# Moving operands of all projections read alternately from two places

## The chip, the cores and the metric

The kernel runs on one core of a Trainium2 chip. The metric is the device time of one execution in microseconds (us), lower is better. The core has five engines that run their own instruction streams: PE (TensorE, matmuls into PSUM, each with a weight load of its own), DVE (VectorE), ACT (ScalarE), POOL (GpSimd) and SP (SyncE, which here issues DMA transfers only).

## The reference

One encoder layer on 256 tokens of width 2048, with 16 learned meta tokens ahead of them (272 positions), all in float32:

```python
u = rms_norm(h, norm_mix[l])
proj = jnp.einsum('bld,dc->blc', u, w_in[l])
aq, ak, av, mq, mk, mv, mo, mg = jnp.split(proj, IN_SPLITS, axis=-1)
...
attn_out = diff_attention(...)
ml_out = mlstm_mixer(...)
mixed = jnp.concatenate([attn_out, ml_out.astype(attn_out.dtype)], axis=-1)
h = h + jnp.einsum('blc,cd->bld', mixed, w_out[l])
u = rms_norm(h, norm_ffn[l])
ff = jax.nn.silu(jnp.einsum('bld,df->blf', u, w_gate[l])) * jnp.einsum('bld,df->blf', u, w_up[l])
h = h + jnp.einsum('blf,fd->bld', ff, w_down[l])
...
h = rms_norm(h, norm_final)
return h[:, N_META:]
```

The head width of the differential attention is 128 (8 heads, two components of 64), that of the mLSTM 256 (4 heads, both directions). D_FF is 5632.

## The kernel before

**Arithmetic.** Every large product is made of three fp32r matmuls. An operand x is split into a high part `xh`, x rounded to fp32r, and a low part `xl`, which is x less `xh`; a product of two split operands is high by high, high by low and low by high. ACT makes the high part (a CAST), DVE or POOL the low part (a subtraction).

**Token operands.** Activations lie with their channels on the 128 partitions and tokens along the row: `uh` and `ul` hold the 16 blocks of the normalised input, 272 tokens each; `mixh[k]` and `mixl[k]` hold the mixed heads, 256 tokens; `vhl` holds high and low of the input of the feed-forward part, side by side, 256 tokens each; `ffh` and `ffl` hold its inner activations. A matmul has a stationary operand (`lhsT`, 128 columns, loaded by a weight load) and a moving one (`rhs`), whose columns stream through PE one after another; the result of moving column n goes to column n of the accumulator in PSUM.

**Projections.** `project` (L209) computes 512 output channels as four accumulators of 128 channels. It walks over the weight matrix in pieces of 256 rows by 512 columns: `load_raw` (L178) transfers a piece (512 KB) on SP's queue, `split_piece` (L195) splits it, and once two pieces are there it issues the matmuls for both. The stationary operand is a 128 by 128 block of the weights, the moving operand a block of the token operand: 272 columns for ak, av, mk and mv, 258 for mq, 256 for aq, mo and the output projection `wo`. With `both`, in gate and up (L1016 to L1042), one matmul of 512 columns multiplies the high weights with high and low tokens at once (L235), and one of 256 the low weights with the high tokens (L236); DVE adds the halves.

**First projection.** aq's first half is written out by hand (L363 to L453), with its instructions pinned: transposes of x, `x_split` (L377), which splits the transposed block out of PSUM into `uh` and `ul`, the splits of the weights, and the matmuls (`aq_matmul`, L394) follow the arrival of x. `meta_columns` (L342) does for the meta tokens what `x_split` does for x, on POOL. `gates` (L532) computes the 16 gate columns from `uh` and `ul` with a moving operand of 272 columns.

**Between the projections** run attention and the mLSTM as generators that `slot` advances. `split_mix` (L807) writes their results into `mixh` (ACT) and `mixl` (POOL). Ahead of the output projection POOL puts x together again as `uh` plus `ul` into `res` (L973). After each group of the output projection DVE adds the accumulator to `res`, ACT and DVE split the sum into `vhl` (L986, L987).

**Down.** Here the roles are turned: the stationary operand is a block of `ffh` or `ffl` (128 tokens), and the moving operand 512 columns of the split weights; `down_mm` (L1061) issues the three matmuls. In the last of the four column groups one accumulator is cut into two of 256 columns. `add_square` (L1072) adds an accumulator to `h2n`, which holds tokens on the partitions, and sums the squares for the last norm.

**Order.** Apart from pinned instructions, a scheduler with a timeline of its own places the instructions of every engine. The rows and their order are the same before and after on PE and SP; on ACT and DVE the rows and their order are the same with other shapes; on POOL two instructions become two pairs.

Of the kernel before, what the change touches and what calls it, by code (L numbers as in the profile page):

```python
# [86 lines left out]
def tile_hybrid_encoder_layer(  # L87
# [42 lines left out]
    def f(ap):  # L130
        return ap.bitcast(F32)
# [77 lines left out]
    def project(src, c0, xh, xl, n, name, kpairs=None, gain=None, hook=None, pre=(), pins=0, both=None):  # L209
        kpairs = list(range(KD // CK)) if kpairs is None else kpairs  # L210
        accs = [acc_tile(f"acc_{name}_{j}") for j in range(4)]
        pend = []
        for i, kp in enumerate(kpairs):
            if hook is not None:
                hook(i)
            elif i % 2 == 0:
                slot()
            if i < len(pre):
                wh, wl = pre[i]
            else:  # L220
                wh, wl = load_piece(src, kp * CK, c0, f"{name}_{kp}", gain, pin if i < pins else unpinned)
            pend.append((i, kp, wh, wl))
            if len(pend) < 2:
                continue
            for j in range(4):
                o = accs[j][:, :n]
                sl = slice(j * P, (j + 1) * P)
                for ii, kq, qh, ql in pend:
                    for kk in range(CK):
                        k = kq * CK + kk  # L230
                        first = ii == 0 and kk == 0
                        last = ii == len(kpairs) - 1 and kk == CK - 1
                        if both is not None:
                            pair = accs[j].rearrange("p (a n) -> p a n", a=2)
                            T.matmul(pair, lhsT=qh[:, kk, sl], rhs=both(k), start=first, stop=False)  # L235
                            T.matmul(pair[:, 1, :], lhsT=ql[:, kk, sl], rhs=xh(k), start=False, stop=last)  # L236
                            continue
                        T.matmul(o, lhsT=qh[:, kk, sl], rhs=xh(k), start=first, stop=False)  # L238
# [103 lines left out]
    def meta_columns():  # L342
        pmv = state["sc"][:, 1, :KD * NM].rearrange("p (k t) -> p k t", t=NM)
        mt = scr[:, 1024:1024 + KD * NM].rearrange("p (k t) -> p k t", t=NM)
        pin(A.copy(mt, pmv))
        G.tensor_copy(uh[:, :, :NM], mt)
        G.tensor_tensor(ul[:, :, :NM], mt, f(uh[:, :, :NM]), ALU.subtract)
        sq = scr[:, 512:512 + KD * NM].rearrange("p (k t) -> p k t", t=NM)
        G.tensor_tensor(sq, mt, mt, ALU.mult)

# [24 lines left out]
                pin(T.transpose(pm[:, m * NM:(m + 1) * NM], mn[:, m * P:(m + 1) * P], ident[:NM, :NM]))  # L375

    def x_split(d):  # L377
        pt = state[d][:, :SEQ]
        pin(A.copy(uh[:, d, NM:], pt))
        pin(V.tensor_tensor(ul[:, d, NM:], pt, f(uh[:, d, NM:]), ALU.subtract))  # L380

    def w_split(k):
        kk = k % CK
# [9 lines left out]

    def aq_matmul(j, k, term):  # L394
        wh, wl = state["wh", k // CK][:, k % CK], state["wl", k // CK][:, k % CK]
        o, sl = accs[j][:, :SEQ], slice(j * P, (j + 1) * P)
        w = wl if term == 2 else wh
        u = ul if term == 1 else uh
        pin(
            T.matmul(  # L400
                o, lhsT=w[:, sl], rhs=u[:, k, NM:],
                start=(k == 0 and term == 0), stop=(k == KD - 1 and term == 2),
            )
        )
# [127 lines left out]
    def gates():  # L532
# [4 lines left out]
        yield  # L537
        pgate = sm_tile("pgate")
        for k in range(KD):
            T.matmul(pgate[:32, :NT], lhsT=wgp[:, k, :], rhs=uh[:, k, :], start=(k == 0), stop=False)  # L540
            T.matmul(pgate[:32, :NT], lhsT=wgp[:, k, :], rhs=ul[:, k, :], start=False, stop=(k == KD - 1))
# [263 lines left out]
        return dst  # L805

    def split_mix(src, k):  # L807
        mixh[k] = kpool.tile([P, SEQ], F32R, tag="qk", bufs=32, name=f"mixh{k}")
        mixl[k] = kpool.tile([P, SEQ], F32R, tag="qk", bufs=32, name=f"mixl{k}")
# [157 lines left out]
    lp1 = left1.__enter__()  # L967
    left2 = tc.tile_pool(name="left2", bufs=1)
    lp2 = left2.__enter__()
    vhl = lp2.tile([P, KD, 2, SEQ], F32R, name="vhl")  # L970
    vh, vl = vhl[:, :, 0, :], vhl[:, :, 1, :]
    res = lp1.tile([P, KD, SEQ], F32, name="res")
    for d in range(KD):  # L973
        G.tensor_tensor(res[:, d, :], f(uh[:, d, NM:]), f(ul[:, d, NM:]), ALU.add)
    ssf = lp2.tile([P, SEQ], F32, name="ssf")
    rbf = lp2.tile([P, SEQ], F32, name="rbf")
    for g in range(4):
        accs = project(
            w_out[0], g * N_CHUNK, lambda k: mixh[k], lambda k: mixl[k], SEQ, f"wo{g}",
        )  # L980
        for j in range(4):
            d = 4 * g + j
            with tc.high_priority():
                V.tensor_tensor(res[:, d, :], accs[j][:, :SEQ], res[:, d, :], ALU.add)
            gcol = cols[:, V_GFFN + d:V_GFFN + d + 1]
            A.activation(vh[:, d, :], res[:, d, :], AF.Copy, scale=gcol)  # L986
            V.scalar_tensor_tensor(vl[:, d, :], res[:, d, :], gcol, f(vh[:, d, :]), ALU.mult, ALU.subtract)  # L987
# [27 lines left out]

    for g in range(D_FF // N_CHUNK):  # L1016
        accs = project(
            w_gate[0], g * N_CHUNK, lambda k: vh[:, k, :], None, SEQ, f"ga{g}",
            both=lambda k: vhl[:, k], hook=ffn_norm if g == 0 else None,
        )  # L1020
        sgs = []
        for j in range(4):
            s1 = fp.tile([P, SEQ], F32, tag="s1", bufs=2, name=f"s1_{g}_{j}")
            sg = fp.tile([P, SEQ], F32, tag="sg", bufs=5, name=f"sg_{g}_{j}")
            with tc.high_priority():
                add_halves(s1, accs[j])
# [4 lines left out]
        accs = project(  # L1031
            w_up[0], g * N_CHUNK, lambda k: vh[:, k, :], None, SEQ, f"up{g}",
            both=lambda k: vhl[:, k],
        )
# [25 lines left out]

    def down_mm(part, k, wh, wl, kk, pin=False):  # L1061
        acc, b, c0, n = part
        o = acc[:, :n]
        bsl = slice(b * P, (b + 1) * P)
        csl = slice(c0, c0 + n)
        mm = T.matmul(o, lhsT=ffh[:, k, bsl], rhs=wh[:, kk, csl], start=(k == 0), stop=False)  # L1066
        if pin:
            tc.keep_in_program_order(mm)
        T.matmul(o, lhsT=ffh[:, k, bsl], rhs=wl[:, kk, csl], start=False, stop=False)  # L1069
        T.matmul(o, lhsT=ffl[:, k, bsl], rhs=wh[:, kk, csl], start=False, stop=(k == KF - 1))  # L1070

    def add_square(part, n0, col):  # L1072
        acc, b, c0, n = part
        ysl = slice(n0 + c0, n0 + c0 + n)
        V.tensor_tensor(h2n[:, b, ysl], acc[:, :n], h2n[:, b, ysl], ALU.add)
# [96 lines left out]
```

## Time and profile before

| | |
|---|---|
| Time, median of 3 runs | 1198.35 us (1198.05 to 1199.13) |
| Time of the profiled execution | 1198.92 us |
| Its span | 1197.1 us |
| PE, weight loads | 7629 records each |
| DVE, ACT, POOL | 1153, 1179, 313 instructions |
| DMA | 212.85 MB, mean 178 GB/s |
| Granted clock of the core, mean | 0.998 |

The profiled execution was recorded by the hardware profiler; the median is of runs without it. Its page gives busy times of each engine, the chain of work that ended last, and groups of instructions by line, operation and tile. "Busy" for PE covers the whole time from the start of a matmul to its modelled end, and successive matmuls overlap, so PE at 99% doesn't say at what pace it works. A group row holds line, engine and operation, output and inputs, active rows and columns, shape, count, then busy time, the mean time of one in ns and the idle time of the engine ahead of it. Some matmul records can be missing from a trace.

The stages by their first and last matmul on the timeline: input projections with attention and mLSTM up to 356 us, output projection to 448 us, gate and up to 939 us, down to 1189 us, and the end of the last norm with the output.

### The profile page before, as it was taken

The page shows a single profiled execution, that of the slowest core. Times are in us where ns is not written, and L with a number is a line of the kernel's source. Part 1 is how long each engine was busy: PE and PEld are TensorE (multiplying, and loading weights), DVE is VectorE, ACT ScalarE, POOL GpSimd, SP SyncE. Part 2 cuts the span into 40 slices and gives each one's busy share as a digit, 9 for nine tenths or more (in the row PEclk, how much of TensorE's full clock was granted, in tenths as well). Part 3 has the DMA queues.
Part 4 walks back from the last instruction along what each step waited for, and adds up shares of the span by engine and source line. Part 5 has one row for each costly group of instructions (what it writes and reads, how often), then busy time and mean ns, then how long its engine had stood idle before and what let it go on. Part 6 is the DMA issues. An engine that isn't in the chain of part 4 may idle for free.

```text
span 1197.1 us, 19833 instructions
## 1 busy us (share of the span) xinstructions
PE 1184.0 (99%) x7629; PEld 1073.5 (90%) x7629; DVE 731.3 (61%) x1153; ACT 649.5 (54%) x1179; POOL 241.6 (20%) x313
## 2 busy tenths in 40 slices
PE   9999999999999999999999999999999999999997
PEld 8999999999999998888888888888888888888896
DVE  6887877887766566555655655665554544444444
ACT  6568768678965344554554454454554534343433
POOL 7220130010227633122122122122132100000000
PEclk9999999999999999999999999999999999999999
DMA  8555455454445655565665665655655755555563
GB/s 270 164 156 160 138 153 150 141 145 139 140 142 178 196 189 178 183 203 177 193 195 177 200 187 177 210 178 176 211 179 174 251 189 186 186 186 185 182 187 103
DMA packets 112255, 212.85 MB, mean 178 GB/s; under 512 B 8906, under 2 KB 9744, under 8 KB 112016
## 3 DMA queue, kind: packets, MB, share of 16 engines
q1 hardware_dynamic: 111664, 210.48, 57.0%
q8 instruction: 60, 0.98, 0.3%
q10 hardware_dynamic: 176, 1.06, 0.3%
q14 instruction: 35, 0.29, 0.1%
q0 software_dynamic: 320, 0.04, 0.0%
HBM read 209.45 MB, written 2.10 MB: 177 GB/s over the span
## 4 chain that ended last, share of the span: by engine, by line
PE 93%; DVE 3%; DMA 1%; ACT 1%; issue 1%; SPq 0%; POOL 0%; ACTq 0%; DVEq 0%; POOLq 0%
PE acc_up L235 14%; PE acc_ga L235 14%; PE acc_ga L236 7%; PE acc_up L236 7%; PE acc_dn L1066 7%; PE acc_dn L1070 7%; PE acc_dn L1069 7%; PE acc_wo L239 3%; PE acc_wo L240 3%; PE acc_wo L238 3%; PE acc_mv L238 1%; PE acc_mv L240 1%; PE acc_mv L239 1%; PE acc_mo L240 1%; PE acc_mo L238 1%; PE acc_mo L239 1%
## 5 line engine op out<-in xcount | busy, mean ns | idle before, releaser
L235 PE MATMUL acc_ga<-vhl,wh_ga 128*128 128x512 f32 x704 | 240.8, 394 | 0.0
L235 PE MATMUL acc_up<-vhl,wh_up 128*128 128x512 f32 x704 | 240.5, 394 | 0.0
L200 DVE TENSOR_TENSOR wl_dn<-raw_dn,wh_dn 128x1024 fp32r<-128x1024 f32 x88 | 108.2, 1230 | 133.3 <-ACT wh_dn L199 133.3
L236 PE MATMUL acc_ga<-vhl,wl_ga 128*128 128x256 f32 x704 | 187.0, 280 | 0.0
L236 PE MATMUL acc_up<-vhl,wl_up 128*128 128x256 f32 x704 | 186.5, 280 | 0.0
L200 DVE TENSOR_TENSOR wl_up<-raw_up,wh_up 128x1024 fp32r<-128x1024 f32 x88 | 115.0, 1337 | 91.0 <-ACT wh_up L199 91.0
L199 ACT CAST wh_dn<-raw_dn 128x1024 fp32r<-128x1024 f32 x88 | 92.2, 1049 | 142.7 <-PE acc_dn L1070 130.9
L200 DVE TENSOR_TENSOR wl_ga<-raw_ga,wh_ga 128x1024 fp32r<-128x1024 f32 x88 | 106.1, 1236 | 79.4 <-ACT wh_ga L199 79.4
L235 PEld LDWEIGHTS acc_ga<-vhl,wh_ga 128*128 128x128 f32 x704 | 129.9, 188 | 26.2
L235 PEld LDWEIGHTS acc_up<-vhl,wh_up 128*128 128x128 f32 x704 | 129.9, 188 | 26.2
L1070 PE MATMUL acc_dn<-wh_dn,ffl 128*128 128x512 f32 (+1 forms) x396 | 146.8, 371 | 0.0
L1066 PE MATMUL acc_dn<-wh_dn,ffh 128*128 128x512 f32 (+1 forms) x396 | 146.7, 371 | 0.0
L1069 PE MATMUL acc_dn<-wl_dn,ffh 128*128 128x512 f32 (+1 forms) x396 | 146.4, 370 | 0.0
L236 PEld LDWEIGHTS acc_up<-vhl,wl_up 128*128 128x128 f32 x704 | 132.2, 189 | 3.8
L236 PEld LDWEIGHTS acc_ga<-vhl,wl_ga 128*128 128x128 f32 x704 | 132.2, 189 | 3.6
L199 ACT CAST wh_ga<-raw_ga 128x1024 fp32r<-128x1024 f32 x88 | 89.1, 1049 | 81.4 <-PE acc_ga L235 41.8
L199 ACT CAST wh_up<-raw_up 128x1024 fp32r<-128x1024 f32 x88 | 89.0, 1048 | 68.9 <-PE acc_ga L235 36.8
L1070 PEld LDWEIGHTS acc_dn<-wh_dn,ffl 128*128 128x128 f32 x396 | 74.5, 188 | 13.7
L1069 PEld LDWEIGHTS acc_dn<-wl_dn,ffh 128*128 128x128 f32 x396 | 74.5, 188 | 13.7
L1066 PEld LDWEIGHTS acc_dn<-wh_dn,ffh 128*128 128x128 f32 x396 | 74.5, 188 | 13.4
L239 PE MATMUL acc_wo<-mixl,wh_wo 128*128 128x256 f32 x256 | 72.2, 282 | 0.0
L240 PE MATMUL acc_wo<-mixh,wl_wo 128*128 128x256 f32 x256 | 71.9, 281 | 0.0
(365 smaller groups left out, 2607.0 us busy)
## 6 DMA issues: line engine op xcount, KB each, us to landing
raw_ga<-in_w_gate_dram SPq DMA_DIRECT2D x88, 512.0 KB, 4.4
raw_up<-in_w_up_dram SPq DMA_DIRECT2D x88, 512.0 KB, 4.5
raw_dn<-in_w_down_dram SPq DMA_DIRECT2D x88, 512.0 KB, 4.2
raw_wo<-in_w_out_dram SPq DMA_DIRECT2D x32, 512.0 KB, 4.0
raw_ak<-in_w_in_dram SPq DMA_DIRECT2D x16, 512.0 KB, 4.2
raw_av<-in_w_in_dram SPq DMA_DIRECT2D x16, 512.0 KB, 4.0
raw_mv<-in_w_in_dram SPq DMA_DIRECT2D x16, 512.0 KB, 3.9
raw_mo<-in_w_in_dram SPq DMA_DIRECT2D x16, 512.0 KB, 4.0
```

The source lines that it names most:

```text
L199: pin(A.copy(wh, raw))
L200: pin(V.tensor_tensor(wl, raw, f(wh), ALU.subtract))
L235: T.matmul(pair, lhsT=qh[:, kk, sl], rhs=both(k), start=first, stop=False)
L236: T.matmul(pair[:, 1, :], lhsT=ql[:, kk, sl], rhs=xh(k), start=False, stop=last)
L238: T.matmul(o, lhsT=qh[:, kk, sl], rhs=xh(k), start=first, stop=False)
L239: T.matmul(o, lhsT=qh[:, kk, sl], rhs=xl(k), start=False, stop=False)
L240: T.matmul(o, lhsT=ql[:, kk, sl], rhs=xh(k), start=False, stop=last)
L1066: mm = T.matmul(o, lhsT=ffh[:, k, bsl], rhs=wh[:, kk, csl], start=(k == 0), stop=False)
L1069: T.matmul(o, lhsT=ffh[:, k, bsl], rhs=wl[:, kk, csl], start=False, stop=False)
L1070: T.matmul(o, lhsT=ffl[:, k, bsl], rhs=wh[:, kk, csl], start=False, stop=(k == KF - 1))
```

## The change

Each token operand is stored as two halves in each of its blocks: even tokens in the first half, odd tokens in the second. `uh` and `ul` get the shape (128, 16, 2, 136), `mixh[k]` and `mixl[k]` (128, 2, 128), `vhl` (128, 16, 2, 2, 128). The matmuls read the halves by turns (`woven`): first token 0 from the first half, then token 1 from the second, then token 2 from the first, 512 or 544 bytes apart. So the accumulators hold the tokens in the old order, and what follows them is as before; only their view is given as pairs. The instructions that write the operands read their source with a step of two words (`apart`) and write the two halves; POOL's two instructions for the meta tokens become two for each half. The sum for `res` reads the halves and writes with a step of two.

In down the storage of the weights stays. A matmul's 512 (or 256) moving columns are read by turns from the left and the right half of the column group (`woven(halves(...))`), 1,024 (or 512) bytes apart, and the accumulator holds the columns in that order; `add_square` reads it with a step of two words and adds it to the two halves of the row of `h2n`.

Stationary operands, the number of matmuls and their columns, transfers and pools stay. The core of the diff:

```diff
-    uh = lowp.tile([P, KD, NT], F32R, name="uh")
-    ul = lowp.tile([P, KD, NT], F32R, name="ul")
+    HT, HM, HS = NT // 2, NM // 2, SEQ // 2
+    uh = lowp.tile([P, KD, 2, HT], F32R, name="uh")
+    ul = lowp.tile([P, KD, 2, HT], F32R, name="ul")
+
+    def woven(ap):
+        return ap.rearrange("p r n -> p n r")
+
+    def pairs(ap):
+        return ap.rearrange("p (n r) -> p n r", r=2)
+
+    def apart(ap):
+        return ap.rearrange("p (n r) -> p r n", r=2)
+
+    def halves(ap):
+        return ap.rearrange("p (r n) -> p r n", r=2)
...
@@ project
-                o = accs[j][:, :n]
+                o = pairs(accs[j][:, :n])
...
-                            pair = accs[j].rearrange("p (a n) -> p a n", a=2)
+                            pair = accs[j].rearrange("p (a n r) -> p a n r", a=2, r=2)
                             T.matmul(pair, lhsT=qh[:, kk, sl], rhs=both(k), start=first, stop=False)
-                            T.matmul(pair[:, 1, :], lhsT=ql[:, kk, sl], rhs=xh(k), start=False, stop=last)
+                            T.matmul(pair[:, 1], lhsT=ql[:, kk, sl], rhs=xh(k), start=False, stop=last)
...
@@ in_proj
-            w_in[0], c0, lambda k: uh[:, k, t0:], lambda k: ul[:, k, t0:], NT - t0, name, gain=gm, **kw
+            w_in[0], c0, lambda k: woven(uh[:, k, :, t0 // 2:]), lambda k: woven(ul[:, k, :, t0 // 2:]),
+            NT - t0, name, gain=gm, **kw
...
@@ meta_columns
-        G.tensor_copy(uh[:, :, :NM], mt)
-        G.tensor_tensor(ul[:, :, :NM], mt, f(uh[:, :, :NM]), ALU.subtract)
+        for r in range(2):
+            G.tensor_copy(uh[:, :, r, :HM], mt[:, :, r::2])
+            G.tensor_tensor(ul[:, :, r, :HM], mt[:, :, r::2], f(uh[:, :, r, :HM]), ALU.subtract)
...
@@ x_split
-        pt = state[d][:, :SEQ]
-        pin(A.copy(uh[:, d, NM:], pt))
-        pin(V.tensor_tensor(ul[:, d, NM:], pt, f(uh[:, d, NM:]), ALU.subtract))
+        pt = apart(state[d][:, :SEQ])
+        pin(A.copy(uh[:, d, :, HM:], pt))
+        pin(V.tensor_tensor(ul[:, d, :, HM:], pt, f(uh[:, d, :, HM:]), ALU.subtract))
...
@@ split_mix
-        A.copy(mixh[k], src)
-        G.tensor_tensor(mixl[k], src, f(mixh[k]), ALU.subtract)
+        A.copy(mixh[k], apart(src))
+        G.tensor_tensor(mixl[k], apart(src), f(mixh[k]), ALU.subtract)
...
-        G.tensor_tensor(res[:, d, :], f(uh[:, d, NM:]), f(ul[:, d, NM:]), ALU.add)
+        G.tensor_tensor(apart(res[:, d, :]), f(uh[:, d, :, HM:]), f(ul[:, d, :, HM:]), ALU.add)
...
-            A.activation(vh[:, d, :], res[:, d, :], AF.Copy, scale=gcol)
-            V.scalar_tensor_tensor(vl[:, d, :], res[:, d, :], gcol, f(vh[:, d, :]), ALU.mult, ALU.subtract)
+            rd = apart(res[:, d, :])
+            A.activation(vh[:, d], rd, AF.Copy, scale=gcol)
+            V.scalar_tensor_tensor(vl[:, d], rd, gcol, f(vh[:, d]), ALU.mult, ALU.subtract)
...
-            w_gate[0], g * N_CHUNK, lambda k: vh[:, k, :], None, SEQ, f"ga{g}",
-            both=lambda k: vhl[:, k], hook=ffn_norm if g == 0 else None,
+            w_gate[0], g * N_CHUNK, lambda k: woven(vh[:, k]), None, SEQ, f"ga{g}",
+            both=lambda k: vhl[:, k].rearrange("p a r n -> p a n r"), hook=ffn_norm if g == 0 else None,
...
@@ down_mm
-        o = acc[:, :n]
+        o = pairs(acc[:, :n])
         bsl = slice(b * P, (b + 1) * P)
-        csl = slice(c0, c0 + n)
-        mm = T.matmul(o, lhsT=ffh[:, k, bsl], rhs=wh[:, kk, csl], start=(k == 0), stop=False)
+        ph, pl = (woven(halves(w[:, kk, c0:c0 + n])) for w in (wh, wl))
+        mm = T.matmul(o, lhsT=ffh[:, k, bsl], rhs=ph, start=(k == 0), stop=False)
...
@@ add_square
-        V.tensor_tensor(h2n[:, b, ysl], acc[:, :n], h2n[:, b, ysl], ALU.add)
+        y = halves(h2n[:, b, ysl])
+        V.tensor_tensor(y, apart(acc[:, :n]), y, ALU.add)
```

The up projection, the output projection, `aq_matmul` and the gate matmuls are changed in the same way as those shown.

More of the change, by code (lines that the diff above doesn't have):

```diff
@@ L395, in aq_matmul @@
         wh, wl = state["wh", k // CK][:, k % CK], state["wl", k // CK][:, k % CK]
-        o, sl = accs[j][:, :SEQ], slice(j * P, (j + 1) * P)
+        o, sl = pairs(accs[j][:, :SEQ]), slice(j * P, (j + 1) * P)
         w = wl if term == 2 else wh
@@ L400, in aq_matmul @@
             T.matmul(
-                o, lhsT=w[:, sl], rhs=u[:, k, NM:],
+                o, lhsT=w[:, sl], rhs=woven(u[:, k, :, HM:]),
                 start=(k == 0 and term == 0), stop=(k == KD - 1 and term == 2),
@@ L539, in gates @@
         for k in range(KD):
-            T.matmul(pgate[:32, :NT], lhsT=wgp[:, k, :], rhs=uh[:, k, :], start=(k == 0), stop=False)
-            T.matmul(pgate[:32, :NT], lhsT=wgp[:, k, :], rhs=ul[:, k, :], start=False, stop=(k == KD - 1))
+            o = pairs(pgate[:32, :NT])
+            T.matmul(o, lhsT=wgp[:, k, :], rhs=woven(uh[:, k]), start=(k == 0), stop=False)
+            T.matmul(o, lhsT=wgp[:, k, :], rhs=woven(ul[:, k]), start=False, stop=(k == KD - 1))
         gsb = kpool.tile([32, NT + 2], F32, tag="t1", bufs=5, name="gsb")
@@ L807, in split_mix @@
     def split_mix(src, k):
-        mixh[k] = kpool.tile([P, SEQ], F32R, tag="qk", bufs=32, name=f"mixh{k}")
-        mixl[k] = kpool.tile([P, SEQ], F32R, tag="qk", bufs=32, name=f"mixl{k}")
-        A.copy(mixh[k], src)
-        G.tensor_tensor(mixl[k], src, f(mixh[k]), ALU.subtract)
+        mixh[k] = kpool.tile([P, 2, HS], F32R, tag="qk", bufs=32, name=f"mixh{k}")
+        mixl[k] = kpool.tile([P, 2, HS], F32R, tag="qk", bufs=32, name=f"mixl{k}")
+        A.copy(mixh[k], apart(src))
+        G.tensor_tensor(mixl[k], apart(src), f(mixh[k]), ALU.subtract)
     def attention(h0, nh):
@@ L969, in tile_hybrid_encoder_layer @@
     lp2 = left2.__enter__()
-    vhl = lp2.tile([P, KD, 2, SEQ], F32R, name="vhl")
-    vh, vl = vhl[:, :, 0, :], vhl[:, :, 1, :]
+    vhl = lp2.tile([P, KD, 2, 2, HS], F32R, name="vhl")
+    vh, vl = vhl[:, :, 0], vhl[:, :, 1]
     res = lp1.tile([P, KD, SEQ], F32, name="res")
     for d in range(KD):
-        G.tensor_tensor(res[:, d, :], f(uh[:, d, NM:]), f(ul[:, d, NM:]), ALU.add)
+        G.tensor_tensor(apart(res[:, d, :]), f(uh[:, d, :, HM:]), f(ul[:, d, :, HM:]), ALU.add)
     ssf = lp2.tile([P, SEQ], F32, name="ssf")
@@ L978, in tile_hybrid_encoder_layer @@
         accs = project(
-            w_out[0], g * N_CHUNK, lambda k: mixh[k], lambda k: mixl[k], SEQ, f"wo{g}",
+            w_out[0], g * N_CHUNK, lambda k: woven(mixh[k]), lambda k: woven(mixl[k]), SEQ, f"wo{g}",
         )
@@ L1031, in tile_hybrid_encoder_layer @@
         accs = project(
-            w_up[0], g * N_CHUNK, lambda k: vh[:, k, :], None, SEQ, f"up{g}",
-            both=lambda k: vhl[:, k],
+            w_up[0], g * N_CHUNK, lambda k: woven(vh[:, k]), None, SEQ, f"up{g}",
+            both=lambda k: vhl[:, k].rearrange("p a r n -> p a n r"),
         )
@@ L1062, in down_mm @@
         acc, b, c0, n = part
-        o = acc[:, :n]
+        o = pairs(acc[:, :n])
         bsl = slice(b * P, (b + 1) * P)
-        csl = slice(c0, c0 + n)
-        mm = T.matmul(o, lhsT=ffh[:, k, bsl], rhs=wh[:, kk, csl], start=(k == 0), stop=False)
+        ph, pl = (woven(halves(w[:, kk, c0:c0 + n])) for w in (wh, wl))
+        mm = T.matmul(o, lhsT=ffh[:, k, bsl], rhs=ph, start=(k == 0), stop=False)
         if pin:
             tc.keep_in_program_order(mm)
-        T.matmul(o, lhsT=ffh[:, k, bsl], rhs=wl[:, kk, csl], start=False, stop=False)
-        T.matmul(o, lhsT=ffl[:, k, bsl], rhs=wh[:, kk, csl], start=False, stop=(k == KF - 1))
+        T.matmul(o, lhsT=ffh[:, k, bsl], rhs=pl, start=False, stop=False)
+        T.matmul(o, lhsT=ffl[:, k, bsl], rhs=ph, start=False, stop=(k == KF - 1))
     def add_square(part, n0, col):
```

## The prediction

> **What bounds the kernel now.** I read the page's busy shares first, then the chain of work that ended last.
>
> ```profile
> PE 1184.0 (99%) x7629; PEld 1073.5 (90%) x7629; DVE 731.3 (61%) x1153; ACT 649.5 (54%) x1179; POOL 241.6 (20%) x313
> ...
> PE 93%; DVE 3%; DMA 1%; ACT 1%; issue 1%; SPq 0%; POOL 0%; ACTq 0%; DVEq 0%; POOLq 0%
> ```
>
> PE (TensorE) is busy for 99% of the span, and 93% of the chain is PE. The profiled execution took 1198.92 us, 0.6 us over the median of the runs (1198.35); the sum below is made against 1198.92. Next, the stretches of the program: input projections with attention and the mLSTM, output projection, gate and up, down. Each row holds the length, then busy time and count (x) of PE, of its weight loads, of DVE, ACT and POOL, then the granted clock, the DMA share and GB/s.
>
> ```profile
> 37.30:356.30 319.00, 317.20 (x2556) 310.73 (x2555) 250.40 (x591) 234.80 (x578) 54.49 (x81) 1.00 0.52 149
> 356.30:447.90 91.60, 91.60 (x778) 91.60 (x777) 58.86 (x70) 43.12 (x60) 51.44 (x51) 1.00 0.57 182
> 447.90:938.80 490.90, 490.90 (x2824) 430.96 (x2823) 280.02 (x320) 240.29 (x353) 102.04 (x135) 1.00 0.60 189
> 938.80:1188.60 249.80, 249.80 (x1218) 207.62 (x1216) 114.35 (x111) 103.10 (x126) 9.75 (x9) 1.00 0.57 180
> ```
>
> PE has no gap in the three later projections, and 1.8 us of gaps in the first (319.00 less 317.20). The clock is 1.00 in all four. Next come the two longest waits of PE.
>
> ```profile
> PE pw L292 <- POOL ones L139: 1.4, 1, 1.4
> PE acc_av L238 <- DVE ak L802: 0.8, 1, 0.8
> ```
>
> None is over 1.4 us. So the time is a number of matmuls times the distance from one start to the next, and only that distance is worth looking at. The timeline of gate, start in us first:
>
> ```profile
> 600.91 0.39 PE L235 MATMUL acc_ga<-vhl,wh_ga 128*128 128x512 f32 x1
> 601.14 0.28 PE L236 MATMUL acc_ga<-vhl,wl_ga 128*128 128x256 f32 x1
> 601.26 0.39 PE L235 MATMUL acc_ga<-vhl,wh_ga 128*128 128x512 f32 x1
> 601.49 0.28 PE L236 MATMUL acc_ga<-vhl,wl_ga 128*128 128x256 f32 x1
> ```
>
> A matmul of 512 columns starts 0.23 us before its successor (600.91 to 601.14, 601.26 to 601.49), one of 256 columns 0.12 (601.14 to 601.26). What do columns cost? The groups by shape give finer numbers; the mean time of one is the last number before the second bar.
>
> ```profile
> L235 PE MATMUL acc_ga<-vhl,wh_ga 128*128 128x512 f32 x704 | 240.8, 394 | 0.0
> L236 PE MATMUL acc_ga<-vhl,wl_ga 128*128 128x256 f32 x704 | 187.0, 280 | 0.0
> ...
> L706 PE MATMUL pst<-mqT,mkT 128*128 128x256 f32 x16 | 4.1, 379 | 0.0
> ...
> L1113 PE MATMUL ph<-ident,res 128*128 128x128 f32 x32 | 5.3, 271 | 0.0
> ```
>
> The recorded duration is the distance plus a constant: 394 less 230 is 164. Taking 164 off all rows, L236 has 116 ns for 256 columns. Then 230 less 116 is 114 ns for the other 256 columns, 0.445 ns a column. L706 and L1113 aren't fp32r but plain fp32, where one instruction leaves several records: 379 less 164 is 215 ns for 256 columns, 271 less 164 is 107 for 128, 0.84 ns a column without any remainder. Half of that is 0.42. So **an fp32r column costs 0.45 ns where the fp32 rows, at half the pace, make 0.42 likely: about 7% of every projection is a stall that grows with the columns**, and is missing where the moving operand is read half as fast. That is the only loss left in PE that I can see.
>
> The Trainium skill, TensorE: Matmul & The Clock Gate, section "Wait — 56ns, not 53.3ns?", states a start-to-start distance of N divided by 2.4 GHz plus about 2.5 ns, 216 ns for 512 columns; the trace disagrees for fp32r (230) and agrees in the fp32 row (215 for 256 columns, a distance that it would give to 512). By it the sum below would be the same within 2 us.
>
> **The change, part by part.** The instructions of every engine stay in their order, and no wait or DMA is added. What changes is where operands lie and in what order they are read.
>
> *1. Matmuls (all of the projections, and the 32 for the gates).* The operand that streams through PE is no longer read from consecutive words. Column 0 comes from one block, column 1 from another 512 to 1,024 bytes away, column 2 from the first again. Counts, stationary operand, PSUM order and number of columns stay. The trace has no matmul that reads this way, so the cost of a column is bounded from both sides by the nearest rows. Below: 0.42 ns (the stall is gone). Above: 0.84 ns (each column costs what it costs in L706, the slowest streaming row). I take the lower end and set out why under the rivals. Distances now, from windows that hold one kind of work:
>
> ```profile
> 360.00:440.00 80.00, 80.00 (x680) 80.00 (x679) 50.71 (x53) 37.67 (x52) 49.02 (x47) 1.00 0.58 184
> 500.00:900.00 400.00, 400.00 (x2301) 351.19 (x2300) 225.61 (x252) 196.20 (x288) 80.87 (x108) 1.00 0.60 189
> 945.00:1125.00 180.00, 180.00 (x785) 145.38 (x784) 81.76 (x70) 72.07 (x82) 5.39 (x4) 1.00 0.60 191
> ```
>
> Gate and up: 400.00 us for 2301 matmuls, 173.8 ns each, 347.7 for a pair of 512 and 256. Output projection: 80.00 by 680 is 117.6 ns. Down: 180.00 us less 20 transposes of 0.107 is 177.9, by 765 is 232.5 ns. The input projections I take from the groups, less 164:
>
> ```profile
> L238 PE MATMUL acc_mv<-uh,wh_mv 128*128 128x272 f32 x128 | 37.5, 294 | 0.0
> ...
> L238 PE MATMUL acc_mo<-uh,wh_mo 128*128 128x256 f32 x128 | 36.2, 283 | 0.0
> ...
> L876 PE MATMUL po<-val,aT 128*128 128x128 f32 x32 | 6.2, 275 | 0.0
> ```
>
> That is 130 ns for 272 columns, stretched where other matmuls come between (by L236, 0.445 ns for each of 16 more columns make 123; I use 127, the middle), and 119 for 256. The matmuls of 258 columns are counted with these, those of 256 in down's tail with the output projection. What stands in the way of 0.42 a column in short matmuls is the weight load that each has: L876, 128 columns with a new stationary operand every time, has 275 less 164, 111 ns, though its columns need 107. I take 111 as the floor of a 256-column matmul, 117 for 272 and 215 for 512. The sum:
> - gate and up: 1408 pairs by (347.7 less 326) 21.7 ns, 30.6 us
> - down, 512 columns: 924 by 17.5 ns, 16.2 us
> - output projection and down's tail: 768 and 264 by 6.6 ns, 6.8 us
> - input projections of 272 columns (ak, av, mk, mv): 1344 by 10 ns, 13.4 us
> - of 256 or 258 (mo, mq, the second half of aq): 768 by 8 ns, 6.1 us; the first half of aq runs while data arrive, and is left out
>
> Together 73.1 us. With 107.5 in place of 111 as the floor (and 114 for 272) each of the 4552 matmuls below 512 columns gives 3.5 ns more: 89.
>
> *2. What covers it.* A faster PE waits for weights. In the first long stretch DVE is busy 250.40 of 319 us; with 24 us less that is 85%, and ACT (234.80) 80%. Between its bursts PE will sometimes wait there; the gaps of today are 1.8 us, and I put 4 more at it. Gate and up leave DVE at 61% of 460 us, down at 50%, and the DMA share rises from 0.60 to 0.64: nothing there becomes the bound. Left, rounded: **70 us**.
>
> *3. Operands written apart.* The splits that write the operands read every second word:
>
> ```profile
> L974 POOL TENSOR_TENSOR res<-uh,ul 128x256 f32<-128x256 f32 x16 | 18.9, 1219 | 0.1
> ...
> L987 DVE SCALAR_TENSOR_TENSOR vhl<-res,cols,vhl 128x256 fp32r<-128x256 f32 x16 | 12.3, 766 | 0.6 <-ACT vhl L986 0.6
> L380 DVE TENSOR_TENSOR ul<-ptx,uh 128x256 fp32r<-128x256 f32 x16 | 6.8, 423 | 3.7 <-ACT uh L379 3.2
> L1075 DVE TENSOR_TENSOR h2n<-acc_dn,h2n 128x512 f32<-128x512 f32 x7 | 4.5, 684 | 3.3 <-PE acc_dn L1070 3.3
> ...
> L986 ACT ACTIVATE vhl<-res,cols 128x256 fp32r<-128x256 f32 x16 | 7.8, 503 | 8.6 <-DVE res L984 8.6
> L379 ACT CAST uh<-ptx 128x256 fp32r<-128x256 f32 x16 | 5.9, 366 | 3.5 <-PE ptx L371 3.5
> ```
>
> Times if each were to take twice as long (the far end; the near end is nothing): L379 and L380 12.7 us in the first 37 us on two engines that are two thirds busy, of which perhaps 3 reach PE; L986 and L987 20.1 us beside the output projection, where DVE has 33 us free of 91.6; L974 18.9 on POOL, needed only at the end of each output group. L1075 is on the path once, at the end, with 0.4 us. I take 0 and keep 4 us for the range. On POOL two instructions become four:
>
> ```profile
> L347 POOL TENSOR_TENSOR ul<-scr,uh 128x256 fp32r<-128x256 f32 x1 | 0.7, 738 | 0.1
> L346 POOL CAST uh<-scr 128x256 fp32r<-128x256 f32 x1 | 0.4, 387 | 0.0
> ```
>
> Half as long each plus a start, so at most 1.1 us more, inside the stretch that waits for x; nothing.
>
> **Rivals.**
>
> *A, forecast: the stall goes.* For it: the loss is proportional to columns (114 against 116 ns for each 256), independent of which tensor is read (gate reads vhl, which nobody writes; down reads weights that ACT and DVE write beside it; 230 against 232.5), and absent at half the reading pace. So it is a limit of reading one place after another, and two places by turns is what could relieve it. 1198.9 less 70 is **1129**. Own range 1110 (floor 107.5) to 1165 (half of the gain).
>
> *B, slower: the second place costs a fetch of its own.* Consecutive words share what is fetched; read by turns, each column might need a fetch. Place: every projection matmul. Price with the far end, 0.84 a column: gate and up 1408 pairs by (645 less 347.7) 419 us; down 924 by 197.5, 182; output projection and down's tail 1032 by 97.4, 101; the input projections 1344 by 101.5 and 960 by 96, 229. Together 931 us: **2130**; if half of the columns pay, 1664. It decides as soon as a column costs over 0.453 ns (347.7 by 768). Against it: PE reads two far places already, the moving operand and the next weights, and the matmuls of 256 columns, which load the same weights in half the time, lose no more per column than those of 512. For it: no row shows a scattered read at full pace. The Trainium skill, SBUF — State Buffer, section "Specifications (TRN2)", speaks for it: lines of 16 bytes need at least two hits for full bandwidth, and each crossing to a new line pays. No row here shows such a crossing by turns; contiguous fp32r crosses every fourth column.
>
> *C, no difference.* The 7% is not in reading the moving operand but, say, in writing PSUM or in an fp32r step of the array. Then only part 3 is left: 1199, up to 1203. For it: the trace cannot tell those from reading, since L706 differs in kind of arithmetic as well as in pace.
>
> *D, a mild loss.* C, and the strided splits cost what part 3 bounds, or PE's short matmuls lose a few ns at the start: 2430 thousand columns are read, and a hundredth more of them is 11 us: 1210.
>
> **How the numbers follow.** A 0.64, with everything down to a small gain; C 0.15; B 0.16; D 0.05. Within 0.2% (2.4 us, about what a measurement of this kernel can tell from no change): 0.15; faster 0.64; slower 0.21. The range reaches from A's lower end, 1110, over C to 1205; it leaves out B, most of D and a little of A, under 2 in 10.
>
> **What would show it.** A: gate's 512 columns near 379 ns recorded in place of 394, its 256 columns near 275, the row of 500 to 900 us with some 2450 matmuls, PE still without gaps after the input projections. B: the same rows near 594 and 379, DVE and ACT half idle. C: rows unchanged to 2 ns. Part 2 is wrong if PE waits for wh and wl by more than 10 us in sum; part 3 if L379, L380 or L987 grow by over a third and a wait for them is among PE's longest. The prediction fails altogether if the stall is the array's own.

## The result and the profile after

The changed kernel takes 1133.8 us (median of 4 runs, 1133.51 to 1134.18) against 1198.46 us for the kernel before, a ratio of 0.946 with a 95% interval of 0.9444 to 0.9477. The profiled execution has a span of 1132.3 us, 64.8 us less than before.

The page's busy times and the chain by engine, of the kernel after:

```profile
PE 1114.3 (98%) x7629; PEld 1043.5 (92%) x7629; DVE 730.0 (64%) x1153; ACT 649.6 (57%) x1179; POOL 244.5 (22%) x315
...
PE 91%; DVE 5%; DMA 2%; issue 1%; ACT 1%; SPq 0%; POOL 0%; ACTq 0%; DVEq 0%; POOLq 0%
```

PE still fills the span. It runs the same 7629 matmul records in less time, so the distance from one start to the next has shrunk on the mean. Where the time went shows in the same stretches as before, cut at the first matmul of each stage (length, then busy time and count of PE, weight loads, DVE, ACT, POOL, then clock, DMA share, GB/s):

```profile
37.60:343.00 305.40, 299.36 (x2556) 292.95 (x2556) 250.00 (x591) 233.19 (x578) 56.19 (x81) 1.00 0.53 156
343.00:429.60 86.60, 86.60 (x778) 86.60 (x777) 59.61 (x70) 44.20 (x60) 53.67 (x51) 1.00 0.60 192
429.60:891.60 462.00, 462.00 (x2824) 424.82 (x2824) 277.13 (x319) 240.52 (x351) 101.47 (x136) 1.00 0.63 201
891.60:1123.70 232.10, 232.10 (x1218) 206.81 (x1216) 115.18 (x112) 103.45 (x128) 9.71 (x10) 1.00 0.60 194
```

Output projection 91.60 to 86.60, gate and up 490.90 to 462.00, down 249.80 to 232.10: 5.0, 28.9 and 17.7 us less, with PE free of gaps in all three as before. The input projections fall from 319.00 to 305.40, while PE's busy time in them falls from 317.20 to 299.36: 17.8 us of work are gone and the gaps grow from 1.8 to 6.0 us. The groups by shape carry the distances (mean time of one in ns ahead of the second bar):

```profile
L248 PE MATMUL acc_ga<-vhl,wh_ga 128*128 128x512 f32 x704 | 227.4, 382 | 0.0
...
L249 PE MATMUL acc_ga<-vhl,wl_ga 128*128 128x256 f32 x704 | 182.1, 273 | 0.0
...
L1083 PE MATMUL acc_dn<-wh_dn,ffh 128*128 128x512 f32 x308 | 117.2, 381 | 0.0
...
L251 PE MATMUL acc_wo<-mixh,wh_wo 128*128 128x256 f32 x256 | 70.3, 275 | 0.0
...
L251 PE MATMUL acc_mv<-uh,wh_mv 128*128 128x272 f32 x128 | 36.2, 284 | 0.0
...
L251 PE MATMUL acc_av<-uh,wh_av 128*128 128x272 f32 x128 | 35.9, 282 | 2.1 <-DVE ak L818 2.0
...
L251 PE MATMUL acc_mo<-uh,wh_mo 128*128 128x256 f32 x128 | 35.4, 277 | 0.0
```

Less 164, as in the prediction, these are 218 ns for 512 columns in gate (230 before), 109 for 256; 217 for 512 columns in down; 111 and 113 for 256 in the output projection and mo; 118 to 120 for 272 in ak, av and mv, where interruptions stretch the mean. An uninterrupted pair of gate and up comes to 327 ns:

```profile
500.00:850.00 350.00, 350.00 (x2140) 321.82 (x2139) 208.00 (x235) 183.48 (x268) 72.96 (x99) 1.00 0.64 202
```

350.00 us by half of 2140. The longest waits of PE, after:

```profile
PE pat L877 <- DVE e L870: 3.0, 2, 1.8
PE acc_av L251 <- DVE ak L818: 2.0, 1, 2.0
PE pw L306 <- POOL ones L139: 1.4, 1, 1.4
PE ptx L386 <- DMA xn<-in_x_dram: 0.9, 1, 0.9
PE acc_aq L415 <- DVE ul L395: 0.5, 1, 0.5
PE acc_av L253 <- DVE wl_av L206: 0.4, 1, 0.4
```

The same wait of the transposes before, at 0.5 us:

```profile
PE pat L861 <- DVE e L854: 0.5, 1, 0.5
```

The new gaps are this wait of the transposes of attention for its softmax weights (`e`), 2.5 us longer, and the one of av's first matmul for the rope of ak, 1.2 us longer; waits for split weights (`wl`) stay below half a microsecond. The groups of the splits that now read with a step of two words:

```profile
L1003 ACT ACTIVATE vhl<-res,cols 128x256 fp32r<-128x256 f32 x16 | 9.2, 595 | 8.7 <-DVE res L1000 8.6
L1004 DVE SCALAR_TENSOR_TENSOR vhl<-res,cols,vhl 128x256 fp32r<-128x256 f32 x16 | 13.1, 820 | 1.0 <-ACT vhl L1003 1.0
L990 POOL TENSOR_TENSOR res<-uh,ul 128x256 f32<-128x256 f32 x16 | 19.6, 1268 | 0.1
L395 DVE TENSOR_TENSOR ul<-ptx,uh 128x256 fp32r<-128x256 f32 x16 | 6.8, 422 | 3.2 <-ACT uh L394 2.4
```

L1003 was 503 ns, L1004 766, L990 1219, L395 423. None is near twice its time.

### The profile page after: what moved, and what is told of

Read it like the earlier page. It is cut to its first block, busy times and chain, and to the rows that moved or that the text cites. A ratio compares the mean times of both kernels' runs of the same rounds, so it can differ in the third digit from the quotient of the medians.

```text
span 1132.3 us, 19840 instructions
## 1 busy us (share of the span) xinstructions
PE 1114.3 (98%) x7629; PEld 1043.5 (92%) x7629; DVE 730.0 (64%) x1153; ACT 649.6 (57%) x1179; POOL 244.5 (22%) x315
## 4 chain that ended last, share of the span: by engine, by line
PE 91%; DVE 5%; DMA 2%; issue 1%; ACT 1%; SPq 0%; POOL 0%; ACTq 0%; DVEq 0%; POOLq 0%
PE acc_up L248 14%; PE acc_ga L248 14%; PE acc_ga L249 7%; PE acc_up L249 7%; PE acc_dn L1086 7%; PE acc_dn L1083 7%; PE acc_dn L1087 7%; PE acc_wo L251 3%; PE acc_wo L252 3%; PE acc_wo L253 3%; PE acc_mv L251 1%; PE acc_mv L252 1%; PE acc_mv L253 1%; PE acc_mo L253 1%; PE acc_mo L251 1%; PE acc_mo L252 1%
## 5 line engine op out<-in xcount | busy, mean ns | idle before, releaser
L248 PE MATMUL acc_ga<-vhl,wh_ga 128*128 128x512 f32 x704 | 227.4, 382 | 0.0
L248 PE MATMUL acc_up<-vhl,wh_up 128*128 128x512 f32 x704 | 227.0, 382 | 0.0
L249 PE MATMUL acc_ga<-vhl,wl_ga 128*128 128x256 f32 x704 | 182.1, 273 | 0.0
L249 PE MATMUL acc_up<-vhl,wl_up 128*128 128x256 f32 x704 | 181.6, 273 | 0.0
L1083 PE MATMUL acc_dn<-wh_dn,ffh 128*128 128x512 f32 (+1 forms) x396 | 141.2, 357 | 0.0
L1087 PE MATMUL acc_dn<-wh_dn,ffl 128*128 128x512 f32 (+1 forms) x396 | 141.2, 357 | 0.0
L1086 PE MATMUL acc_dn<-wl_dn,ffh 128*128 128x512 f32 (+1 forms) x396 | 140.9, 356 | 0.0
L212 ACT CAST wh_up<-raw_up 128x1024 fp32r<-128x1024 f32 x88 | 88.8, 1047 | 57.0 <-PE acc_ga L248 30.6
L1057 POOL TENSOR_TENSOR sg<-up,sg 128x256 f32<-128x256 f32 x44 | 33.4, 759 | 174.1 <-DVE up L1031 174.0
```

Source lines behind the costliest of these rows:

```text
L212: pin(A.copy(wh, raw))
L249: T.matmul(pair[:, 1], lhsT=ql[:, kk, sl], rhs=xh(k), start=False, stop=last)
L1083: mm = T.matmul(o, lhsT=ffh[:, k, bsl], rhs=ph, start=(k == 0), stop=False)
L1086: T.matmul(o, lhsT=ffh[:, k, bsl], rhs=pl, start=False, stop=False)
L1087: T.matmul(o, lhsT=ffl[:, k, bsl], rhs=ph, start=False, stop=(k == KF - 1))
```

## The experiments

The stages show that reading by turns is faster. They don't show why, and three explanations fit them: that successive columns come from places that lie apart (theory "place" below), that the operand is described in several dimensions ("form"), or that each new line of memory costs something and two lines can stay open ("line"). In down the order of the moving columns can be chosen freely in each of four column groups, since the storage of the weights stays and the addition of the accumulator undoes the order. So each kernel of the first kind below has three orders in the first three groups (of 264 matmuls of 512 columns each) and leaves the rest of the kernel after as it is. PE does the same arithmetic and writes PSUM in the same order in all of them. Each of these five kernels was run once; the groups of one run are compared with each other and with the distances above. What is compared is the mean distance between starts: the length of a window inside the group, by three times the count of one of the three lines, good to one per cent. (The recorded duration of the slow orders is longer than the distance by more than 164, so it isn't used.)

**Plain, in pairs, 8 bytes apart.** Written out for the third group (the kernel takes the order of each group from a table):

```diff
@@ down_mm
-        ph, pl = (woven(halves(w[:, kk, c0:c0 + n])) for w in (wh, wl))
+        ph, pl = (w[:, kk, c0:c0 + n].rearrange("p (n r j) -> p n j r", r=2, j=2) for w in (wh, wl))
@@ add_square
-        V.tensor_tensor(y, apart(acc[:, :n]), y, ALU.add)
+        V.tensor_tensor(y, acc[:, :n].rearrange("p (n j r) -> p n r j", r=2, j=2), y, ALU.add)
```

where `y` has the form "p n r j" too. The others differ in r and j only.

> The kernel after, with another reading order in the first three column groups of down (the fourth stays as after): group 0 reads its 512 moving columns plainly, as before; group 1 reads the same consecutive words, but described in pairs (steps 2 and 1); group 2 reads words 0, 2, 1, 3 of every four, so the two places lie 8 bytes apart. Theory 'place' (the stall comes from consecutive columns lying in the same small unit of memory): group 0 at 232 ns a matmul, group 1 the same 232, group 2 still near 232 as long as the unit is 16 bytes or more. Theory 'form' (an operand described in several dimensions escapes the stall): 232, 216, 216. Whole kernel: place 1133.8 plus 3 times 4.4 is 1147, form 1138.

The three rows of this kernel, one for each group, from windows of 60 us (892 to 952), 57 us (957 to 1014) and 57 us (1019 to 1076):

```profile
L1130 PE MATMUL acc_dn<-wh_dn,ffh 128*128 128x512 f32 x86 | 33.9, 396 | 0.0
L1130 PE MATMUL acc_dn<-wh_dn,ffh 128*128 128x512 f32 x81 | 32.1, 396 | 0.0
L1130 PE MATMUL acc_dn<-wh_dn,ffh 128*128 128x512 f32 x82 | 32.5, 396 | 0.0
```

60 us by 258 is 233 ns, 57 by 243 is 235, 57 by 246 is 232; the kernel took 1147.3 us. With the first three groups back at the old distance the kernel is 13.5 us slower than after. The second group tells nothing new: pairs that follow one another were merged, and its operand is the same plain row of 512 words. The third is a real operand of three dimensions, whose columns also come from two places by turns, and it is as slow as plain reading. "Form" falls, and with it the idea that any two places read by turns would do: 8 bytes are too near. "Place" had expected this.

**16, 32 and 64 bytes apart** (j = 4, 8, 16 in the diff above).

> As the run with 8 bytes, with the two places 16, 32 and 64 bytes apart in groups 0, 1 and 2 of down. Theory 'place': 216 ns a matmul from the distance on that is larger than the unit; if the unit is a line of 16 bytes (the Trainium skill, SBUF — State Buffer, names such lines) all three groups are at 216, if it is larger the first one or two stay at 232. Theory 'line' (each new line costs, two places only escape because their lines stay open): 216 in all three. Theory 'form': 216 in all three. Whole kernel 1134 to 1143.

The first two groups, from windows of 56 us each (892 to 948, 950 to 1006); the row of the third (1008 to 1064) reads like the second's:

```profile
L1130 PE MATMUL acc_dn<-wh_dn,ffh 128*128 128x512 f32 x86 | 32.5, 380 | 0.0
L1130 PE MATMUL acc_dn<-wh_dn,ffh 128*128 128x512 f32 x87 | 33.1, 380 | 0.0
```

56 us by 258 is 217 ns, by 261 it is 215, and the kernel took 1133.8 us, as after. From 16 bytes on it makes no difference how far apart the places lie. For "place" this would make the unit 16 bytes; "line" had expected 216 ns here too.

**128 bytes apart; a step of 8; a step of 16 bytes.** The second group reads all even words and then all odd ones, the third every fourth word in four passes (again written out):

```diff
@@ down_mm
+        # r = 256, j = 2 (second group); r = 128, j = 4 (third group)
+        ph, pl = (w[:, kk, c0:c0 + n].rearrange("p (r j) -> p j r", r=r) for w in (wh, wl))
```

> Group 0 of down: two places 128 bytes apart. Group 1: words read with a step of two (8 bytes), first all even, then all odd. Group 2: words read with a step of four (16 bytes), four passes, so every column lies in a new 16-byte line and none is read twice in a row. Theory 'place': 216 in group 0; in groups 1 and 2 consecutive columns leave the unit sooner than plain reading does, so 216 to 232 in group 1 and 216 in group 2. Theory 'line': 216 in group 0, 232 or more in group 1, and about 430 in group 2 (the kernel then takes 57 us longer, 1191). Theory 'form': 216 in all.

Windows of 55 us (892 to 947), 117 us (950 to 1067) and 119 us (1071 to 1190):

```profile
L1130 PE MATMUL acc_dn<-wh_dn,ffh 128*128 128x512 f32 x84 | 31.8, 380 | 0.0
L1130 PE MATMUL acc_dn<-wh_dn,ffh 128*128 128x512 f32 x86 | 55.7, 648 | 0.0
L1130 PE MATMUL acc_dn<-wh_dn,ffh 128*128 128x512 f32 x86 | 57.0, 663 | 0.0
```

55 us by 252 is 218 ns; 117 by 258 is 453; 119 by 258 is 461. The kernel took 1261.1 us. Theory "place" expected 216 to 232 ns for the step of 8 and 216 for the step of 16, and is wrong by a factor of two. "Line" had 232 or more and about 430, and 1191 us for the kernel: it foresaw that the step of 16 would be slow, not that the step of 8 would be as slow. A step of two words halves the pace, although it touches each line of 16 bytes twice in a row, just as plain reading touches it four times.

**Four places; runs of two words; a step of 32 bytes** (r = 4, j = 128; two places 1,024 bytes apart, two words at a time; r = 64, j = 8 in groups of 512).

> Group 0 of down: four places by turns, 512 bytes apart. Group 1: two places 1,024 bytes apart... read in runs of two words (256 bytes of words each side in turn of 8 bytes). Group 2: a step of eight words (32 bytes). Theory 'place': 216 in group 0 and 216 in group 2; in group 1 every second column still follows its neighbour, so half of the stall, about 224. Theory 'line': 430 in group 2, 216 or more in group 0 if only two lines stay open. Theory 'form': 216 in all.

Windows of 72 us (892 to 964), 84 us (967 to 1051) and 111 us (1055 to 1166):

```profile
L1130 PE MATMUL acc_dn<-wh_dn,ffh 128*128 128x512 f32 x86 | 38.2, 446 | 0.0
L1130 PE MATMUL acc_dn<-wh_dn,ffh 128*128 128x512 f32 x86 | 43.1, 502 | 0.0
L1130 PE MATMUL acc_dn<-wh_dn,ffh 128*128 128x512 f32 x86 | 53.4, 621 | 0.0
```

279, 326 and 430 ns; the kernel took 1236.7 us. "Place" had 216, about 224 and 216, and misses all three; "line" had the 430. The runs of two words are the telling row: only two places are open, and still it is 50% slower than after (326 against 217).

These four kernels suggested a new theory, which the next one was made to test: even and odd columns are fetched by a reader each. With two readers most orders sort themselves by one number, how many words of a line of 16 bytes one reader takes in a row. Plain reading gives words 0 and 2 of a line to one reader, 1 and 3 to the other: two. The order 0, 2, 1, 3 gives 0 and 1 to one, 2 and 3 to the other: two again. By turns from places 16 bytes apart or more: four. A step of 8 bytes: words 0, 4, 8 to one reader, one of each line. Two orders don't fit: with four places, and with runs of two words, a reader takes one word and comes to the same line again later, and they took 279 and 326 ns, far less than the 453 of the step of 8. In this theory the unit has to be 16 bytes: with units of 8, plain reading and the step of 8 would be alike (one word each), with units of 32, plain reading and places 16 bytes apart (four words each).

**Runs of four words; by turns with a step of 8; by turns with a step of 16 bytes.** Shortened:

```diff
@@ down_mm
+        # first group: "r n w" read as "n r w", r = 2, w = 4
+        # second and third group: "r n m" read as "m n r", r = 2, m = 2 or 4
+        held, read, sizes = ...  # of the group
+        ph, pl = (w[:, kk, c0:c0 + n].rearrange(f"p ({held}) -> p {read}", **sizes) for w in (wh, wl))
```

> Two theories are left after the first four kernels. 'Lanes': even columns and odd columns are fetched apart, each by a reader of its own that holds one line of 16 bytes; a column is free of stall where its reader takes all four words of a line in a row, costs about 0.45 ns with two words in a row, and about 0.87 with one. 'Two places': what counts is that each column lies far from the one before it and that no more than two places are visited by turns. The kernel after, with three other orders in down. Group 0: two places 1,024 bytes apart, read in runs of four words; each reader takes two words of a line in a row. Lanes: 232 ns a matmul, as in plain reading. Two places: more than 216 and like the runs of two words (327) or between. Group 1: two places by turns, each read with a step of two words (8 bytes); each reader takes two words of a line in a row. Lanes: 232. Two places: 216. Group 2: two places by turns, each read with a step of four words (16 bytes); each reader takes one word of a line. Lanes: about 450. Two places: 216. Whole kernel: lanes 1134 plus 4.2, 4.2 and 62, that is 1204; two places 1134 to 1163.

Windows of 64 us (893 to 957), 59 us (960 to 1019) and 116 us (1023 to 1139):

```profile
L1087 PE MATMUL acc_dn<-wh_dn,ffh 128*128 128x512 f32 x86 | 35.6, 416 | 0.0
L1087 PE MATMUL acc_dn<-wh_dn,ffh 128*128 128x512 f32 x84 | 33.3, 396 | 0.0
L1087 PE MATMUL acc_dn<-wh_dn,ffh 128*128 128x512 f32 x86 | 55.7, 647 | 0.0
```

64 us by 258 is 248 ns, 59 by 252 is 234, 116 by 258 is 450; the kernel took 1210.7 us. The second and third group read from two places by turns, 1,024 bytes apart, exactly as after does, only with larger steps within each place. Theory "two places" had 216 for both; they came out at 234 and 450, as "lanes" had it. The first group is 7% slower than the 232 that "lanes" expected, and the kernel 7 us slower than its 1204.

All orders together, with the words of a line that one reader takes in a row:

| order of the 512 columns | words in a row per reader | ns |
|---|---|---|
| two places by turns, 16 to 128 or 1,024 bytes apart | 4 | 215 to 218 |
| plain; 0, 2, 1, 3 | 2 | 232 to 235 |
| two places by turns, step of 8 bytes in each | 2 | 234 |
| runs of four words from two places by turns | 2, next line far away | 248 |
| four places by turns | 1, returns to the line | 279 |
| runs of two words from two places by turns | 1, returns to the line | 326 |
| step of 32 bytes | 1 | 430 |
| two places by turns, step of 16 bytes in each | 1 | 450 |
| step of 8 bytes, of 16 bytes | 1 | 453, 461 |

One reader with one open line is excluded: reading by turns would be its worst case. One reader with two open lines is excluded by the runs of two words. The three rows between 240 and 330 ns, in which a reader leaves a line and goes to a distant one, are explained by neither theory in size (by the prices of "lanes" they would be at 232 and twice at about 450), and what they cost was not settled. So it is shown that the order of reading sets the distance; that two readers with a line each are behind it is inferred from the times, with these three rows open, and no record shows the readers.

**Down alone.** The kernel before, with `woven(halves(...))` in `down_mm` and the matching addition in `add_square`, all else as before.

```diff
@@ down_mm of the kernel before
-        csl = slice(c0, c0 + n)
+        ph, pl = (woven(halves(w[:, kk, c0:c0 + n])) for w in (wh, wl))
```

> The kernel before, with only the moving operands of down read by turns; token operands and the other projections as before. The gain of each stage stands by itself: the down stage falls from 249.8 us to 232.1 as in the whole change, nothing else moves, 1198.5 less 17.7 is 1180.8 us, ratio 0.985. Rival: part of down's gain hangs on the earlier stages (its first weights arrive sooner, or the DMA has less to catch up), then the stage is longer than 233 us and the kernel over 1182.

1181.2 us (1180.79 to 1181.68), ratio 0.9856 with an interval of 0.9839 to 0.9872. The stage in one row:

```profile
939.00:1171.10 232.10, 232.10 (x1218) 206.74 (x1216) 114.32 (x110) 102.88 (x126) 9.57 (x9) 1.00 0.59 193
```

It is 232.1 us long, the same as in the whole change.

**Gate and up alone.** The kernel before, with `vhl` in halves, its two splits and the operands of the two projections.

```diff
@@ the kernel before
-    vhl = lp2.tile([P, KD, 2, SEQ], F32R, name="vhl")
+    vhl = lp2.tile([P, KD, 2, 2, SEQ // 2], F32R, name="vhl")
...
-            both=lambda k: vhl[:, k], hook=ffn_norm if g == 0 else None,
+            both=lambda k: vhl[:, k].rearrange("p a r n -> p a n r"), hook=ffn_norm if g == 0 else None,
```

> The kernel before, with only the operand of gate and up stored in halves and read by turns. If the gains add up: the gate and up stage falls from 490.9 to 462.0 us, the output projection keeps its 91.6 us although ACT and DVE write the halves there, and the kernel takes 1198.5 less 28.9, 1169.6 us, ratio 0.976. If the strided splits reach PE, the output projection grows by more than 1 us.

1170.1 us (1169.5 to 1170.4), ratio 0.9763 with an interval of 0.9749 to 0.9778. Input projections, output projection, gate and up, down:

```profile
37.40:356.50 319.10, 317.24 (x2557) 310.76 (x2555) 250.44 (x591) 235.49 (x578) 54.55 (x81) 1.00 0.51 149
356.50:448.10 91.60, 91.60 (x779) 91.60 (x778) 59.19 (x69) 43.54 (x60) 51.57 (x51) 1.00 0.56 182
448.10:910.10 462.00, 462.00 (x2825) 424.81 (x2824) 277.47 (x318) 240.86 (x351) 100.78 (x135) 1.00 0.63 200
910.10:1160.00 249.90, 249.90 (x1218) 207.27 (x1216) 115.09 (x112) 103.97 (x128) 9.98 (x10) 1.00 0.55 181
```

Gate and up take the 462.0 us of the whole change, and the output projection, in which ACT and DVE write the halves, keeps its 91.60 us. The gains of these two stages stand by themselves (output and input projections weren't run alone), and the splits into `vhl` cost PE nothing there.

## Why the prediction was right, point by point

**The bound and its size.** The prediction read the time as a number of matmuls times the distance between their starts, took 7% of that distance for a stall that grows with the columns, and put 73.1 us on its going. By stages: gate and up 30.6 against 28.9 measured; down 17.9 with its tail against 17.7; output projection 5.1 against 5.0; input projections 19.5 against 17.8. Together 69.4. The lower end of 0.42 ns a column, worked out from the fp32 rows at half the pace, was the right end: 512 columns take 217 ns in down and 218 in gate where 215 was set. The floor of 111 ns for short matmuls, from the row of L876, is what the runs of short ones show (275 less 164 in the output projection); beside a matmul of 512 columns they do 109. That the weight load sets this floor, as the prediction says, no run shows: the short matmuls of gate have a weight load each, too. And of the two rows behind the 0.84 ns only L706 leaves several records for one matmul (16 for 8); the 32 transposes of L1113 leave one each. The figure is the same in both.

**The mis-sized terms** are gate and up, and the input projections, 1.7 us each. A pair of gate came down to 327.1 ns where 326 was set (its long matmul 3 ns over the term, its short one 2 under), and 1.1 by 1408 is 1.6 us. In the input projections the recorded means of the 272 columns fell by 9.6 ns where 10 was set, 12.9 us in sum, and those of 256 and 258 columns by 6.4 where 8 was set, 4.9 us: together the 17.8. In mo, 283 became 277. The prediction had taken an uninterrupted 111 from a mean of 119 that interruptions stretch, and they stretch it still (277 less 164 is 113). The 3.7 us by which 69.4 falls short of 73.1, and 0.9 from rounding up to 70, make most of the 5 us between 1129 and 1133.8.

**What covers it.** 4 us of new waits were set for the input projections, and 4.2 came (gaps of 6.0 less 1.8). The size was right and the place was not: PE waits there for attention's softmax and a rope, not for the split weights that the prediction named. (Its 24 us off this stretch don't follow from its own sum, which has 19.5; nothing hangs on them.)

**Operands written apart.** Taken as 0, and no cost to PE is seen: the output projection has no gap after the change, and in the kernel with gate and up alone it keeps its length. In the whole change ACT's split into `vhl` grows by 92 ns, DVE's by 54, POOL's sum by 49, that of x_split not at all. With gate and up alone, where these two have the same form, they grow by 38 and 20 (to 541 and 786 ns), so their step of two words doesn't account for all of the growth; the rest was not traced.

**The reason given for A** was half right. The stall does lie in reading, not in PSUM or the array (rival C): all the kernels of the first kind do the same arithmetic into the same places of PSUM, and their distances run from 215 to 461 ns. But "two places by turns" is not what relieves it. Two places by turns with a step of 8 bytes keep the stall, and with a step of 16 bytes they are as slow as rival B said. As far as the times tell, what the change does is to let each of two readers take four words of a line in a row where plain reading gives it two. The prediction had nothing by which to tell its order from those slow ones; that the order chosen reached the full pace is in part luck.

**Rival B** was a real mechanism with nearly the right price (430 against 430 to 461 measured where each reader takes one word of each line). Its condition was wrong, a fetch for each column, and so was the argument against it, that weights and moving operand are read from far places anyway: that says nothing of one operand. The sentence of the Trainium skill beside it, SBUF — State Buffer, section "Specifications (TRN2)", that a line of 16 bytes needs at least two hits for full bandwidth, agrees with these runs in the unit of 16 bytes. It doesn't agree in the number: a step of 8 bytes hits each line twice in a row and has half the pace (453 ns). Counted per reader, one hit gives half the pace, two give 93%, and only four give all of it. Read as a rule against any order that leaves a line after each column, it would have forecast the wrong sign.

The Trainium skill's other sentence, TensorE: Matmul & The Clock Gate, section "Wait — 56ns, not 53.3ns?", 216 ns for 512 columns, disagreed with the fp32r rows before (230) and agrees with down after (217). That the sum by it would be the same within 2 us holds for the 512 columns alone; with its 109 ns for 256 columns and 116 for 272 the sum is some 79 us, an estimate. Its agreement with the fp32 row of 256 columns needs a plain fp32 column to count as two, which no run here shows.

## What to carry to other kernels

Where PE has no gaps, compare the distance between matmul starts per column with the fastest row in the same trace; a difference that grows with the columns is worth a look at how the moving operand lies in memory. For fp32r operands, reading two blocks 16 bytes or more apart by turns took 5 to 7% off the matmuls of 512 columns, and in down it took no other storage, only views. A plain step in such an operand is to be kept away from: a step of two words doubled the distance (453 ns against 232 for plain reading).

## What the hardware showed that was not expected

- Plain reading of fp32r words is not the fastest order: 232 ns against 216 for 512 columns at a granted clock of 1.00.
- A step of 8 bytes in the moving operand costs as much as one of 16 or 32 (453, 461, 430 ns), while the order 0, 2, 1, 3 costs what plain reading does (232).
- The distance between two places read by turns made no difference at 16, 32, 64, 128 and 1,024 bytes (215 to 218 ns), but 8 bytes are too near (232).
